# Three late modulation sums moved from VectorE, after the attention, to ScalarE products and adding transfers onto DRAM, during it

## The chip, the cores and the metric

The kernel runs on one core of a Trainium2 chip. The metric is the device time of one launch in microseconds, the median of three runs. The engines are TensorE (PE, with its weight loads as PEld), VectorE (DVE), ScalarE (ACT), GpSimd (POOL) and SyncE (SP), which issues most transfers. Each engine works through its own queue in order.

## The reference

A decoder block on 512 tokens of width 1024, in float32. A conditioning vector gives six modulation rows of 1024 numbers, parts 0 to 5:

```
mod = silu(c) @ w_ada + b_ada
shift1, scale1, gate1, shift2, scale2, gate2 = split(mod, 6)
h = rms_norm(x, g_pre_mix) * (1 + scale1) + shift1
y = token_mixer(h)                      # conv branch, attention branch, gates, w_out
x = x + gate1 * rms_norm(y, g_post_mix)
h = rms_norm(x, g_pre_mlp) * (1 + scale2) + shift2
y = square(relu(h @ w_mlp_in)) @ w_mlp_out
x = x + gate2 * rms_norm(y, g_post_mlp)
```

The token mixer projects h with `w_in`. One branch is a gated unit, a causal depthwise convolution of 31 taps, LayerNorm, swish and `w_conv_out`. The other is attention with eight heads over low-rank queries and keys, then `w_attn_out`. Sigmoid gates merge them and `w_out` follows. Parts 2, 3 and 4 (gate1, shift2, scale2) are what the change is about. They are first used after the output projection.

## The kernel before, in words

Tokens stand in four tiles of 128, the width in eight tiles of 128. Nearly every matrix product is done as three matmuls of high and low halves (`mm3`, line 476), so each weight block that arrives from DRAM is cast on ScalarE and its remainder is formed on VectorE (`W`, line 494). SBUF holds two arenas, `f_arena` (22400 words a partition) and `r_arena` (28000), from which buffers are taken and freed.

The program does not issue instructions as it is written. Helpers record every operation in a planner (line 170; line 410 issues them all, which is why nearly every row of the profile names L410). The planner knows each operation's dependences, a cost, and a due time worked back from TensorE's order (lines 329 to 338). It then plays the engines forward: TensorE keeps the recorded order (moved by `boost`); every other engine takes, whenever it is free, the ready operation with the earliest due time less its `hurry` (lines 345 to 377). An operation may also be tied to an earlier one through `after` (line 318). Transfers are costed at lines 237, 238 and 282 to 286 and 363 to 368; those of GpSimd count double. Buffers are placed by the lives of the plan before it, so a place is used again about 1.5 us after the plan lets it go (`Arena.alloc`, line 90). Up to 14 plans are made and the shortest is issued.

The order of the work: the first modulation and the first gated-unit tiles; the latent projection (`lat_gemm`, line 854); the other gated-unit tiles; the attention (lines 1147 to 1162), where for each head the projection of a later head, the scores of the next and the values of this one alternate; then `w_attn_out`, the second gate, the first gate, the LayerNorm, `w_conv_out`, the output projection, the second modulation and the MLP. The convolution is 248 VectorE steps. `pump` (line 836) records a few at a time among the matrix products: 6 after each piece of the latent projection, 20 after each pair of gated-unit tiles, 7 after each head. GpSimd is used for a few small powers, such as the LayerNorm's (line 1282), and for the adding transfers onto `y_spill` in the MLP (line 1716).

Parts 2, 3 and 4 are summed by `ada_units` (line 1167). A unit is 256 rows of `w_ada` for one part, a load of 1 MB into 2048 words. VectorE multiplies each of its two 128-row halves by a column of `cT` and adds it to an accumulator of 128x1024; a part is four units. What remains, a sum over the 128 partitions, is done in `late_mod` (line 1359): for part 2 by a matmul with ones in `gate_row`, for parts 3 and 4 by transposes and a reduction. The units are drawn by `take` at lines 1239, 1316, 1332 and 1399, in the first gate's product, before the LayerNorm's end and in the merge. Part 5 is summed in the same way in the MLP.

Of the kernel before, what the change touches and what calls it, by code (L numbers as in the profile page):

```python
# [11 lines left out]
F32 = mybir.dt.float32  # L12
# [3 lines left out]
ALU = mybir.AluOpType  # L16

P = 128
T = 512
NT = T // P  # L20
D = 1024
KD = D // P
H = 8
# [17 lines left out]
PUMPS = (6, 10, 7, 6, 5)  # L41
# [8 lines left out]
LEAD = 15000.0  # L50
SLOW = 4000.0
ADAS = (1, 1, 0, 4)
KGRP = ((2,), (3,), (4,), (5,), (6,), (7,))
HX, HA, HG, HC = 1.2e5, 1e5, 3e3, 1.1e5

# [359 lines left out]
def tile_hybrid_block(  # L415
# [12 lines left out]
    out = out[0]  # L428
    w_ada, w_in, conv_w, w_conv_out = w_ada[0], w_in[0], conv_w[0], w_conv_out[0]
# [14 lines left out]
        return tiles[name]  # L444

    hD = [tc.dram_tile([P, KD * T], F32, name=f"h_spill{i}") for i in range(2)]
    yD = [tc.dram_tile([P, D], F32, name=f"y_spill{t}") for t in range(NT)]
    ident = const.tile([P, P], F32, name="ident")
    make_identity(nc, ident)
# [14 lines left out]
    def emit(past, replay):  # L464
        fa = Arena(FT, F_WORDS, past.get("f_arena"), replay.get("f_arena"))
        ra = Arena(RT, R_WORDS, past.get("r_arena"), replay.get("r_arena"))
        pb = Banks(PT, past.get("psum"), replay.get("psum"))
        plan = Planner(nc, dict(f_arena=fa, r_arena=ra, psum=pb))
        pe, act, dve, pool, sp = (plan.engine(e) for e in Planner.NAMES)
# [19 lines left out]
        def load(words, src, pat=None, **kw):  # L489
            b = fa.alloc(words)  # L490
            sp.dma_start(out=fa.v(b, pat, **kw), in_=src)
            return b
# [73 lines left out]
        for t in range(NT):  # L566
            b = fa.alloc(D)
# [268 lines left out]
        def pump(n):  # L836
            for _ in range(n):
                if conv_done[0] >= len(conv_seq):
                    return
                g = next(g for g in CONV_DVE if conv_seq[conv_done[0]] in g)  # L840
                if any(ct not in upad for ct in g):
                    return
                next(conv_it)
                conv_done[0] += 1
# [130 lines left out]
        def rope_half(g):  # L975
            wb = fa.alloc(3 * 4 * DR)
            wv = fa.v(wb, "p (k h c) -> p k h c", k=3, h=4)
            for k in range(3):
                sp.dma_start(out=wv[:, k],
                             in_=w_uq[k * P:(k + 1) * P, :].rearrange("p (h c) -> p h c", c=DN + DR)[:, 4 * g:4 * g + 4, DN:])  # L980
            w = W(fa.v(wb, "p (k n) -> p k n", k=3), 3, 4 * DR)
            fa.free(wb)
            qd = []
            for tp in range(2):
                b = pb.alloc()
                for t in range(2):
                    for k in range(3):
                        mm3(pb.v(b)[:, t * 256:(t + 1) * 256], lat(k, (2 * tp + t) * P, P), w(k, 0, 256), k == 0, k == 2)
                q = fa.alloc(512)
                rope(fa.v(q, "p (m s i) -> p m s i", s=2, i=NR), pb.v(b, 512, "p (t m i) -> p t m i", t=2, i=NR), 2 * tp, 2, 4)  # L990
                pb.free(b)
                qd.append(q)
            w.free()

            for hp in range(2):
                b = pb.alloc()
                for t in range(NT):
                    at = (t % 2) * 256 + hp * P
                    pe.transpose(pb.v(b)[:, t * P:(t + 1) * P], fa.v(qd[t // 2])[:, at:at + P], ident)
                for o in range(2):  # L1000
                    q = ra.alloc(T)
                    me, other = slice(o * DR, (o + 1) * DR), slice((1 - o) * DR, (2 - o) * DR)
                    act.copy(ra.v(q)[me], pb.v(b)[me])
                    dve.tensor_tensor(ra.v(q)[other], pb.v(b)[me], rf(q)[me], ALU.subtract)
                    qst[4 * g + 2 * hp + o] = q
                pb.free(b)
            fa.free(*qd)
# [38 lines left out]
        def proj(h):  # L1046
            pr, o = h // 2, h % 2
            if o == 0:
                weights_pair(pr)
            b = pb.alloc()  # L1050
            for k in range(3):
                mm3(pb.v(b), wq[pr](k, o * DN, DN), lat(k), k == 0, k == 2)
            qh, ql = pair(T)
            split(pb.v(b), qh, ql)
            pb.free(b)
            b = pb.alloc()
            for k in range(2):
                mm3(pb.v(b), wkv[pr](k, o * 256, DN), lat(3 + k), k == 0, k == 1)
            kh, kl = pair(T)
            split(pb.v(b), kh, kl)  # L1060
            pb.free(b)
            qkh[h] = (qh, ql, kh, kl)
            if o == 1:
                wq[pr].free()
            if o == 0:
                v_pair(pr)
            else:
                wkv[pr].free()

        def scores(h):  # L1070
            qh, ql, kh, kl = qkh[h]
            sm = []
            for i in range(NT):
                n = (i + 1) * P
                sl = slice(i * P, n)
                b = pb.alloc()
                o = pb.v(b, n)
                mm3(o, (ra.v(qh)[:, sl], ra.v(ql)[:, sl]), (ra.v(kh)[:, :n], ra.v(kl)[:, :n]), True, False)
                pe.matmul(o, lhsT=ra.v(qst[h])[:, sl], rhs=ra.v(K1)[:, :n], start=False, stop=False)
                pe.matmul(o, lhsT=ra.v(qst[h])[:, sl], rhs=ra.v(K2)[:, :n], start=False, stop=True)  # L1080
                s = fa.alloc(n)
                f = fa.alloc(8)
                fv = fa.v(f)
                dve.tensor_tensor_reduce(fa.v(s), o, mask[:, T - n:], 1.0, 3.0e38, ALU.add, ALU.min, fv[:, 0:1])
                pb.free(b)
                act.activation(fa.v(s), fa.v(s), AF.Exp, scale=-1.0, bias=fv[:, 0:1], accum_out=fv[:, 1:2])
                dve.reciprocal(fv[:, 2:3], fv[:, 1:2])
                act.mul(fa.v(s), fa.v(s), fv[:, 2:3])
                fa.free(f)
                sm.append(s)  # L1090
            ra.free(qst[h])
            ra.free(qh, ql, kh, kl)
            sms[h] = sm
# [50 lines left out]
                else:  # L1144
                    ra.free(vh, vl)

        rope_half(0)
        proj(0)
        proj(1)
        scores(0)  # L1150
        for h in range(H):
            if h + 2 < H:
                proj(h + 2)
            if h == 2:
                rope_half(1)
            if h + 1 < H:
                scores(h + 1)
            pv(h)
            pump(PUMPS[2])
        for q in qkv:  # L1160
            ra.free(*q)
        ra.free(K1, K2)


        ada_acc = {}

        def ada_units(parts):

            for part in parts:
                acc = ada_acc[part] = fa.alloc(D)  # L1170
                for u in range(4):
                    b = fa.alloc(2 * D)
                    v = fa.v(b, "p (j n) -> p j n", j=2)
                    sp.dma_start(out=v, in_=w_ada[u * 256:(u + 1) * 256, part * D:(part + 1) * D].rearrange("(j p) n -> p j n", p=P))
                    for jj in range(2):
                        j = u * 2 + jj
                        if j == 0:
                            dve.tensor_scalar(fa.v(acc), v[:, jj], cT[:, 0:1], None, ALU.mult)
                        else:
                            dve.scalar_tensor_tensor(fa.v(acc), v[:, jj], cT[:, j:j + 1], fa.v(acc), op0=ALU.mult, op1=ALU.add)  # L1180
                    fa.free(b)
                    yield

        def take(it, n=100):
            for _ in range(n):
                if next(it, it) is it:
                    return

        late = ada_units((2, 3, 4))


        def feat_gemm(wsrc, c0, rhs, evac, pumped=0, groups=(2, 2, 2, 2)):
# [41 lines left out]
        def ga_evac(ct, b):  # L1234
            t_ = fa.alloc(T)
            act.activation(fa.v(t_), pb.v(b), AF.Tanh, scale=0.5)
            ta.append(t_)
            if ct % 2:
                take(late, ADAS[2])

        feat_gemm(w_in, C_GB, hs, gb_evac, pumped=PUMPS[4])
        pump(KD * TAPS)
        vT = []
# [69 lines left out]
        plan.boost = 0  # L1313
        feat_gemm(w_in, C_GA, hs, ga_evac)
        free_h()
        take(late, ADAS[3])
        plan.boost = 3000
        layer_norm()
        plan.boost = 0
# [4 lines left out]
        def co_evac(ct, b):  # L1324
            m = fa.alloc(T)
            dve.scalar_tensor_tensor(fa.v(m), fa.v(ta[ct]), 1.0, pb.v(b), op0=ALU.add, op1=ALU.mult)
            dve.tensor_tensor(fa.v(m), fa.v(m), fa.v(yb[ct]), ALU.add)
            hl = pair(T)
            split(fa.v(m), *hl)
            mT.append(hl)  # L1330
            fa.free(m, ta[ct], yb[ct])
            take(late, ADAS[0])

        feat_gemm(w_conv_out, 0, lambda k: (ra.v(vT[k][0]), ra.v(vT[k][1])), co_evac, groups=(4, 2, 2))
        for hl in vT:
# [57 lines left out]
        for k0 in range(0, KD, 2):  # L1393
# [2 lines left out]
                for t in range(NT):  # L1396
                    mm3(pb.v(ys[t, 0]), yl(t, k0 + k), w(k, 0, 512), k0 + k == 0, k0 + k == KD - 1)
            w.free()
        take(late)
        G1 = late_mod()  # L1400
        ys.update({(t, 1): pb.alloc() for t in range(NT)})
        wo = [wunit(w_out, k0, 512, 2, 512) for k0 in range(0, KD, 2)]
# [398 lines left out]
```

## Time and profile before

| | |
|---|---|
| median of 3 runs | 813.99 us (813.33 to 814.12) |
| profiled execution | 812.54 us, of it the span 810.4 us |
| busy PE, DVE | 790.7 us, 738.0 us |
| busy ACT, POOL | 472.0 us, 62.8 us |
| granted TensorE clock | 0.998 |
| moved by DMA | 131.00 MB, mean 162 GB/s |

The profile is one execution. Times inside it count from the span's first instruction. A group row gives engine, operation, what is written and read, shapes and count, then busy time in us and mean ns, then the idle time just before these instructions and what ended most of it. The attention's scores lie at about 166 to 244 us, the LayerNorm's power at 358 us, the loads of `w_ada` for parts 2 to 4 at 346 to 404 us and for part 5 at 633 to 651 us.

### The profile page before, as it was taken

How to read it: one execution, taken by the hardware profiler on the slowest of the kernel's cores; microseconds unless marked ns; L12 is line 12 of the kernel's file. 1: busy time of each engine (PE TensorE's matmuls, PEld its weight loads, DVE VectorE, ACT ScalarE, POOL GpSimd, SP SyncE). 2: the span in 40 equal slices, each digit the busy share in tenths (PEclk: the TensorE clock that was granted, in tenths of full speed). 3: DMA queues.
4: the chain of work that ended last, by engine and by line, in shares of the span. 5: the costliest groups of instructions: out<-in, count | busy, mean ns of one | idle time of the engine just before them, and what ended most of it. 6: DMA issues, size and time to landing. Idle time of an engine off the chain costs nothing. (4 is left out here: it accounts for less than half of the span.)

```text
span 810.4 us, 11974 instructions
## 1 busy us (share of the span) xinstructions
PE 790.7 (98%) x4450; PEld 687.7 (85%) x4450; DVE 738.0 (91%) x1045; ACT 472.0 (58%) x784; POOL 62.8 (8%) x121
## 2 busy tenths in 40 slices
PE   6999999999999999999999999999999999999996
PEld 3778988889897888888888879988998899889985
DVE  3898999999999999999997579899689999996997
ACT  5455463365885247229243378677667756777851
POOL 2001010000000000000000021001002200320023
PEclk9999999999999999999999999999999999999999
DMA  9989433112352160064998044159317991895076
GB/s 295 313 247 341 144 116 110 53 53 66 105 170 78 53 202 5 1 222 162 344 391 281 7 159 148 53 149 266 132 53 157 243 343 37 171 288 178 28 164 134
DMA packets 99981, 131.00 MB, mean 162 GB/s; under 512 B 8433, under 2 KB 67154, under 8 KB 99922
## 3 DMA queue, kind: packets, MB, share of 16 engines
q1 hardware_dynamic: 93586, 118.69, 45.1%
q0 software_dynamic: 6336, 11.54, 8.9%
q8 instruction: 35, 0.57, 0.3%
q14 instruction: 24, 0.20, 0.1%
HBM read 109.23 MB, written 20.97 MB: 161 GB/s over the span
## 5 line engine op out<-in xcount | busy, mean ns | idle before, releaser
L410 PE MATMUL psum<-r_arena 128*128 128x512 f32 (+3 forms) x4108 | 751.1, 344 | 4.0 <-DVE f_arena L410 1.6
L410 PEld LDWEIGHTS psum<-r_arena 128*128 128x128 f32 x4108 | 647.6, 189 | 91.7 <-ACT r_arena L410 2.7
L410 ACT CAST r_arena<-f_arena 128x1024 fp32r<-128x1024 f32 (+5 forms) x249 | 235.2, 966 | 137.3 <-PE psum L410 86.4
L410 DVE TENSOR_TENSOR r_arena<-f_arena,r_arena 128x1024 fp32r<-128x1024 f32 (+5 forms) x259 | 276.1, 1093 | 28.0 <-PE psum L410 15.1
L410 DVE SCALAR_TENSOR_TENSOR f_arena<-f_arena,cw 128x512 f32<-128x512 f32 x240 | 164.2, 737 | 0.0
L410 DVE TENSOR_TENSOR f_arena<-f_arena 128x1024 f32<-128x1024 f32 (+3 forms) x108 | 113.6, 1071 | 4.7 <-ACT f_arena L410 2.4
L410 ACT ACTIVATE f_arena<-f_arena 128x512 f32<-128x512 f32 (+4 forms) x121 | 71.3, 607 | 42.9 <-DVE f_arena L410 42.0
L410 ACT COPY f_arena<-psum 128x512 f32<-128x512 f32 (+4 forms) x103 | 55.3, 547 | 41.5 <-PE psum L410 36.9
L410 DVE SCALAR_TENSOR_TENSOR f_arena<-f_arena,cT 128x256 f32<-128x256 f32 (+1 forms) x70 | 55.9, 800 | 1.2
L410 POOL DMA_DIRECT2D y_spill<-f_arena x40 | 34.8, 879 | 263.6 <-ACT f_arena L410 254.8
L410 ACT ACTIVATE f_arena<-psum 128x512 f32<-128x512 f32 x43 | 25.2, 593 | 45.4 <-PE psum L410 44.3
L410 PE MATMUL psum<-ident,f_arena 128*128 128x128 f32 (+1 forms) x234 | 34.8, 288 | 7.9 <-DVE f_arena L410 7.9
L410 PEld LDWEIGHTS psum<-ident,f_arena 128*128 128x128 f32 (+1 forms) x234 | 28.3, 147 | 14.0 <-DVE f_arena L410 9.3
L410 ACT CAST r_arena<-psum 128x512 fp32r<-128x512 f32 (+2 forms) x57 | 30.0, 562 | 12.7 <-PE psum L410 12.4
L410 DVE TENSOR_TENSOR r_arena<-psum,r_arena 128x512 fp32r<-128x512 f32 (+2 forms) x57 | 35.6, 653 | 0.9 <-ACT r_arena L410 0.6
L410 DVE TENSOR_TENSOR f_arena<-psum,f_arena 128x512 f32<-128x512 f32 (+1 forms) x34 | 22.3, 666 | 7.7 <-PE psum L410 7.6
L410 POOL TENSOR_TENSOR stats<-stats,nhalf 128x1 f32<-128x1 f32 (+1 forms) x17 | 15.5, 915 | 172.3 <-ACT stats L410 156.3
L410 POOL TENSOR_TENSOR lns<-lns,nhalf 128x4 f32<-128x4 f32 x1 | 1.4, 1400 | 249.5 <-DVE lns L410 249.5
L410 ACT ACTIVATE r_arena<-f_arena 128x256 fp32r<-128x256 f32 (+3 forms) x17 | 10.9, 642 | 14.4 <-DVE f_arena L410 11.3
L410 ACT ACTIVATE r_arena<-f_arena,mod 128x512 fp32r<-128x512 f32 x8 | 6.5, 816 | 21.6 <-DVE mod L410 21.6
L410 DVE TENSOR_SCALAR f_arena<-f_arena,stats 128x1024 f32<-128x1024 f32 x8 | 6.0, 753 | 13.6 <-POOL stats L410 13.6
L410 DVE CUSTOM_DVE_ANT_0 f_arena<-psum,mask 128x128 f32<-128x128 f32 (+3 forms) x32 | 14.6, 481 | 0.0
(98 smaller groups left out, 211.1 us busy)
## 6 DMA issues: line engine op xcount, KB each, us to landing
f_arena<-in_w_ada_dram SPq DMA_DIRECT2D x16, 1024.0 KB
f_arena<-in_w_mlp_in_dram SPq DMA_DIRECT2D x32, 512.0 KB
f_arena<-in_w_mlp_out_dram SPq DMA_DIRECT2D x32, 512.0 KB
f_arena<-in_w_in_dram SPq DMA_DIRECT2D x24, 512.0 KB
y_spill<-f_arena POOLq DMA_DIRECT2D x40, 256.0 KB, 6.2
f_arena<-in_w_ada_dram SPq DMA_DIRECT2D x32, 256.0 KB
f_arena<-in_x_dram SPq DMA_DIRECT2D x8, 512.0 KB
h_spill<-r_arena SPq DMA_DIRECT2D x16, 256.0 KB
```

Of the source, the lines that this page charges most:

```text
L410: getattr(self.real[o.eng], o.fn)(*o.a, **o.k)
```

## The change

Parts 2, 3 and 4 are now summed by `ada_sums`, drawn in the attention's loop, one or two units a head (`ADAQ`). A unit is loaded as before. ScalarE multiplies each half in place by its column of `cT`. The first half of a part is stored to a tensor in DRAM (`a_spill`) by SP, and each of the seven others is added onto it there by an adding transfer that GpSimd issues, 512 KB each. The buffer is then freed. A unit's load is tied to the last operation recorded before it, and the unit's operations have 50 us of hurry. Before `late_mod` the three sums are loaded back into SBUF, 512 KB each. The calls of `take` at the four old places are gone; part 5 is left as it was.

```
+ADAQ = (1, 1, 1, 2, 2, 2, 2, 1)
+ADAH = 5e4
...
+    aD = {q: tc.dram_tile([P, D], F32, name=f"a_spill{q}") for q in (2, 3, 4)}
...
+        def ada_sums(parts):
+
+            for part in parts:
+                for u in range(4):
+                    plan.hurry, plan.after = ADAH, len(plan.ops) - 1
+                    b = fa.alloc(2 * D)
+                    v = fa.v(b, "p (j n) -> p j n", j=2)
+                    sp.dma_start(out=v, in_=w_ada[u * 256:(u + 1) * 256, part * D:(part + 1) * D].rearrange("(j p) n -> p j n", p=P))
+                    plan.after = None
+                    for jj in range(2):
+                        j = u * 2 + jj
+                        act.mul(v[:, jj], v[:, jj], cT[:, j:j + 1])
+                        if j == 0:
+                            sp.dma_start(out=aD[part], in_=v[:, jj])
+                        else:
+                            pool.dma_start(out=aD[part], in_=v[:, jj], accum_op=ALU.add)
+                    fa.free(b)
+                    plan.hurry = 0.0
+                    yield
...
-        late = ada_units((2, 3, 4))
+        late = ada_sums((2, 3, 4))
...
             pv(h)
             pump(PUMPS[2])
+            take(late, ADAQ[h])
...
-            if ct % 2:
-                take(late, ADAS[2])
-
...
-        take(late, ADAS[3])
...
-            take(late, ADAS[0])
...
-        take(late)
+        for part in (2, 3, 4):
+            ada_acc[part] = load(D, aD[part])
         G1 = late_mod()
```

More of the change, by code (lines that the diff above doesn't have):

```diff
@@ L1145, in pv @@
                     ra.free(vh, vl)
[L1147 to L1162, printed above, removed]
         ada_acc = {}
@@ L1187, in take @@
                     return
-        late = ada_units((2, 3, 4))
+        late = ada_sums((2, 3, 4))
+        rope_half(0)
+        proj(0)
+        proj(1)
+        scores(0)
+        for h in range(H):
+            if h + 2 < H:
+                proj(h + 2)
+            if h == 2:
+                rope_half(1)
+            if h + 1 < H:
+                scores(h + 1)
+            pv(h)
+            pump(PUMPS[2])
+            take(late, ADAQ[h])
+        for q in qkv:
+            ra.free(*q)
+        ra.free(K1, K2)
         def feat_gemm(wsrc, c0, rhs, evac, pumped=0, groups=(2, 2, 2, 2)):
```

## The prediction

> **What bounds the kernel now.** I read the page first (busy time of each engine), then the busy time by stretches of 25 us from the attention to the second modulation, then who TensorE waited for, and last the groups that the change touches.
>
> ```profile
> PE 790.7 (98%) x4450; PEld 687.7 (85%) x4450; DVE 738.0 (91%) x1045; ACT 472.0 (58%) x784; POOL 62.8 (8%) x121
> ```
>
> TensorE is busy in 98% of the span. A busy PE can still run below its pace, so I look at how many matmuls it gets through. The columns are stretch, length, then busy time and instructions of PE, PEld, DVE, ACT and POOL, the granted clock, the DMA share and GB/s.
>
> ```profile
> 150.00:175.00 25.00, 25.00 (x163) 22.91 (x162) 24.30 (x49) 12.92 (x27) 0.00 (x0) 1.00 0.20 64
> 175.00:200.00 25.00, 24.39 (x158) 21.94 (x157) 25.00 (x60) 17.09 (x40) 0.00 (x0) 1.00 0.14 43
> 200.00:225.00 25.00, 24.79 (x159) 22.09 (x159) 24.77 (x60) 17.40 (x42) 0.00 (x0) 1.00 0.30 95
> 225.00:250.00 25.00, 24.65 (x148) 21.38 (x147) 25.00 (x66) 23.29 (x57) 0.00 (x0) 1.00 0.47 141
> 250.00:275.00 25.00, 25.00 (x111) 20.48 (x110) 24.89 (x36) 7.71 (x10) 0.00 (x0) 1.00 0.29 81
> ...
> 350.00:375.00 25.00, 25.00 (x122) 20.64 (x121) 23.90 (x49) 13.94 (x28) 1.40 (x1) 1.00 0.60 213
> 375.00:400.00 25.00, 25.00 (x112) 20.69 (x111) 24.76 (x30) 14.67 (x22) 0.00 (x0) 1.00 0.78 264
> 400.00:425.00 25.00, 25.00 (x112) 20.72 (x111) 24.82 (x31) 8.86 (x11) 0.00 (x0) 1.00 1.02 383
> 425.00:450.00 25.00, 25.00 (x112) 20.71 (x111) 14.73 (x16) 8.41 (x9) 0.00 (x0) 1.00 0.72 235
> 450.00:475.00 25.00, 24.71 (x125) 20.21 (x125) 16.36 (x22) 10.84 (x30) 3.51 (x5) 1.00 0.11 43
> 475.00:500.00 25.00, 23.34 (x175) 21.93 (x174) 22.58 (x35) 21.66 (x47) 4.30 (x4) 1.00 0.63 212
> ```
>
> ```profile
> L410 PE MATMUL psum<-r_arena 128*128 128x512 f32 x332 | 75.4, 389 | 0.0
> ```
>
> The second fence is PE's only group in 375 to 450: all 512-column matmuls, 332 in 75 us, 226 ns apiece. The stretches show the point on which I build: PE does 112 of them in each of 375-400, 400-425 and 425-450, although VectorE is busy for 24.76 and 24.82 us in the first two and for 14.73 us in the third. There VectorE does not set TensorE's pace. Where PE does stand still is in the attention (0.61 + 0.21 + 0.35 = 1.17 us in 175-250) and after the output projection (0.29 + 1.66 = 1.95 us in 450-500). Whom it waited for there, the attention first:
>
> ```profile
> PE psum L410 <- ACT r_arena L410: 0.8, 2, 0.6
> PE psum L410 <- ACT f_arena L410: 0.3, 1, 0.3
> ```
>
> ```profile
> PE psum L410 <- ACT f_arena L410: 1.1, 1, 1.1
> PE psum L410 <- DVE f_arena L410: 0.5, 2, 0.3
> PE psum L410 <- DVE r_arena L410: 0.3, 1, 0.3
> ```
>
> In the attention it waits for ScalarE, the engine that the change loads.
>
> **What the change removes.** VectorE's products for parts 2, 3 and 4, all between 350 and 430:
>
> ```profile
> L410 DVE SCALAR_TENSOR_TENSOR f_arena<-f_arena,cT 128x1024 f32<-128x1024 f32 x21 | 26.8, 1279 | 0.2
> ...
> L410 DVE TENSOR_SCALAR f_arena<-f_arena,cT 128x1024 f32<-128x1024 f32 x3 | 2.2, 748 | 0.2 <-DMA f_arena<-in_w_ada_dram 0.2
> ```
>
> That is 26.8 + 2.2 = 29.0 us of VectorE. By the three equal stretches it is worth 0 to TensorE; what hides it is PE's own queue of ready matmuls. The twelve 1 MB loads leave this stage too, where the DMA share reaches 1.02, but PE did not stop there either: 0. The waits of 450-500 come from the row norms and the eviction of the transposed h, with VectorE busy only 16.36 and 22.58 of 25 us, and those steps stay. A gain there can only come from the planner's new order; its bound is the 1.95 us, with the attention's 1.17 us 3.1 us in all.
>
> **What it adds to ScalarE.** 24 in-place products of 128x1024 by a column of scalars. The nearest rows are the softmax's scalings and a 1024-wide square:
>
> ```profile
> L410 ACT ACTIVATE f_arena<-f_arena 128x384 f32<-128x384 f32 x16 | 9.8, 612 | 1.1 <-DVE f_arena L410 1.1
> ...
> L410 ACT ACTIVATE f_arena<-f_arena 128x256 f32<-128x256 f32 x16 | 8.0, 501 | 0.9 <-DVE f_arena L410 0.9
> ...
> L410 ACT ACTIVATE f_arena<-f_arena 128x1024 f32<-128x1024 f32 x4 | 4.2, 1061 | 7.4 <-DVE f_arena L410 7.4
> ```
>
> From 501 to 612 ns for 128 more columns is 0.87 ns a column, so 612 + 640 x 0.87 = 1.17 us; the square says 1.06. I take 1.16, near the upper end: 24 x 1.16 = 27.8 us. When they come: a unit's load is tied in the plan to the last operation recorded before it, the convolution step that ends the head's pump. 70 steps are recorded ahead of the attention (5 x 6 in the latent GEMM, 2 x 20 in the GLU loop) and 7 a head, so the heads' ties are steps 77, 84, ... 126. The convolution's VectorE time and steps by stretch (stretch, length, busy and count, clock, DMA, GB/s):
>
> ```profile
> 50.00:75.00 25.00, 1.01 (x3) 1.00 0.85 270
> 75.00:100.00 25.00, 21.04 (x32) 1.00 0.57 200
> 100.00:125.00 25.00, 17.02 (x26) 1.00 0.30 95
> 125.00:150.00 25.00, 15.96 (x24) 1.00 0.39 111
> 150.00:175.00 25.00, 8.95 (x14) 1.00 0.20 64
> 175.00:200.00 25.00, 11.45 (x18) 1.00 0.14 43
> 200.00:225.00 25.00, 7.67 (x11) 1.00 0.30 95
> ```
>
> 85 steps are done by 150, 99 by 175, 117 by 200 and 128 by 225. So heads 0 and 1 release their units before 150, and all twelve are released by about 225. ScalarE's idle time from 150 to 275 is 12.08 + 7.91 + 7.60 + 1.71 + 17.29 = 46.6 us, against 27.8 us to be placed. They fit, but each, once begun, holds back the cast or exponential behind it for up to 1.16 us, and a load that lands late would hold ScalarE's whole queue. The price lies between 0 (all in gaps where ScalarE waits) and 27.8 us (each delays TensorE in full). The planner gives ready attention work its place by due time, PE's own waits there are 1.17 us, and 46.6 is well over 27.8, so I take a value near the low end: 0.5 us, less than half of one product. If that cover goes, see the first rival.
>
> **What it adds to the queues.** SP: the twelve loads move ahead of the reloads of h and the gate weights; three plain stores and, before the second modulation, three 0.5 MB reloads are new. They take SP little, and PE waits for no load in 150-250 above: 0. GpSimd: 21 adding transfers of 512 KB, of which those of one part must wait for each other's landing. Rows: GpSimd's issues now, their landing over the whole run, the queue shares, and the only other thing on GpSimd's queue in this stage, the LayerNorm's power (358.4).
>
> ```profile
> L410 POOL DMA_DIRECT2D y_spill<-f_arena x40: 856/862/1117, 536.2 to 787.0; - x40
> ...
> DMA to landing us min/median/max: 3.6/6.2/9.9
> ```
>
> ```profile
> q1 hardware_dynamic: 93586, 118.69, 45.1%
> q0 software_dynamic: 6336, 11.54, 8.9%
> ```
>
> ```profile
> L410 POOL TENSOR_TENSOR lns<-lns,nhalf x1: 1400/1400/1400, 358.4 to 358.4; 128x4 f32<-128x4 f32 x1
> ```
>
> 256 KB lands in 3.6 to 9.9 us, median 6.2. The adding queue used 8.9% of 810.4 us for 11.54 MB, 6.25 us a MB, so another 256 KB costs 1.6 us: 5.2 us for a piece at the least, 6.2 + 1.6 = 7.8 in the median, 2 x 6.2 = 12.4 if it scales. I take 7.8, since the change itself raises the DMA share: 12.6 MB of loads at 3.08 us a MB (45.1% of 810.4 for 118.69 MB) and 11.0 MB of additions at 6.25 make 108 us over some 165. From about 150 the chain then ends at 150 + 21 x 7.8 = 314, 44 us ahead of the power and over 100 ahead of the reloads. Cost 0, with that margin as its cover.
>
> One rule of the Trainium skill speaks against adding from GpSimd's queue: "SBUF — State Buffer", in its box on the "DVE blocks DMA" trap, says that GpSimd can't write a transfer's descriptors while VectorE runs an instruction in a 2-port mode, and gives about 620 ns alone against about 3100 ns beside a copy. By that page a piece would take 2.5 us more, an estimate of 10.3 us. The trace so far disagrees for this kernel's mix: the 40 issues take 856 to 1117 ns beside a VectorE that is busy for most of that time.
>
> **The sum.** 812.54 us is the profiled execution (span 810.4, 2.1 around it), 1.45 under the median of 813.99. 812.54 - 0 (VectorE) - 0 (DMA) + 0.5 (ScalarE) + 0 (queues) = 813.0, on the median's scale 814.5. A measurement of this kernel can tell about 0.2% from no change, 1.6 us.
>
> **The rivals.** First, slower through ScalarE's order: five of the twelve units (heads 5 to 7) are released in about 198-227, ten products, 11.6 us, where ScalarE has 7.60 + 1.71 = 9.3 us idle from 200 to 250. The overflow of 2.3 us delays the last heads' softmax; if as much is lost in the earlier heads, 4.6 us. 816.3 to 818.6. It decides from two products (2.3 us) that fall straight ahead of what PE waits for. For it: PE's attention waits are all on ScalarE. Against it: 17.29 us of idle time lie just behind, and the planner puts due work first. Chance 0.20.
>
> Second, slower through a buffer: the planner's own rule (lines 282 to 286 and 364 to 366) lets a unit's buffer go 4.9 us after the adding transfer is issued, against my 7.8. Each piece adds 2.9 us of lag, and the next tenant, a load or a softmax tile, waits. One or two such waits on the path: 817 to 820. Chance 0.07.
>
> Third, the chain overruns the LayerNorm. From (358.4 - 150) / 21 = 9.9 us a piece on, the power waits behind additions on GpSimd's queue and all of TensorE with it. At 12.4 us the chain ends at 410, 52 us late, 866; issues that are starved by VectorE lead there as well. By the skill's rule above, 10.3 us a piece would end at 366, 8 us late, about 822. Against it: lone pieces of half the size land in 3.6 us. Chance 0.05.
>
> Fourth, faster: the new order, with more room in the arena and idle VectorE and queues after 350, removes most of the 3.1 us of waits, 810.9 to 812.4. Against it: they hang on ScalarE and the norms, which stay. Chance 0.22. That the planner puts the products behind 250, out of the attention, is possible; there ScalarE is mostly idle, and it gives the forecast.
>
> **How the numbers follow.** No measurable change holds 0.46, its own range 812.4 to 815.6; faster 0.22; slower 0.20 + 0.07 + 0.05 = 0.32. The range 811.0 to 819.0 takes in nearly all of the faster case and the first rival, part of the second, and leaves the third out.
>
> **What would show it.** In the profile after: VectorE about 29 us lighter, all of it in 350-430, while the stretches there still count 112 matmuls; ScalarE about 28 us heavier in 140-275 at 1.1 to 1.2 us a product; PE's idle time in 150-250 near 1.2 to 1.7 us (over 3 says the first rival); additions landing in 5 to 10 us, the last before 330, and the power near 358. I am wrong if VectorE's relief raises PE's count anywhere, if ScalarE waits for a late load in the attention, or if the power is late.

## The result and the profile after

The changed kernel takes 834.85 us (median of 4 runs, 833.90 to 835.78), against 813.97 for the kernel before on the same occasion. The ratio is 1.0258, with a 95% interval from 1.0240 to 1.0276: 2.6% slower, 20.9 us. Its profiled execution took 835.78 us, with a span of 834.0.

The page's first line, busy time of each engine:

```profile
PE 796.3 (95%) x4450; PEld 690.0 (83%) x4450; DVE 713.4 (86%) x1021; ACT 495.6 (59%) x808; POOL 83.5 (10%) x142
```

VectorE is 24.6 us lighter (738.0 before) and ScalarE 23.6 us heavier (472.0), a few us short of the 29 and 28 that were forecast. TensorE's share has fallen from 98 to 95%. The stretches of 25 us show where; the columns are as in the prediction:

```profile
150.00:175.00 25.00, 25.00 (x158) 22.60 (x157) 24.76 (x50) 18.32 (x32) 3.44 (x4) 1.00 0.69 163
175.00:200.00 25.00, 18.36 (x104) 15.98 (x103) 17.30 (x42) 15.40 (x33) 1.72 (x2) 0.86 0.71 164
200.00:225.00 25.00, 25.00 (x169) 22.82 (x168) 24.77 (x57) 19.72 (x42) 2.59 (x3) 1.00 0.74 193
225.00:250.00 25.00, 23.79 (x150) 21.08 (x149) 23.65 (x60) 22.72 (x52) 2.16 (x3) 1.00 0.92 269
250.00:275.00 25.00, 23.74 (x116) 18.21 (x115) 20.92 (x42) 17.36 (x35) 1.30 (x2) 1.00 0.93 278
...
300.00:325.00 25.00, 17.76 (x79) 14.37 (x77) 21.01 (x26) 10.76 (x13) 2.13 (x3) 0.92 0.96 273
...
400.00:425.00 25.00, 25.00 (x112) 20.71 (x111) 8.37 (x9) 10.94 (x15) 0.00 (x0) 1.00 0.52 171
425.00:450.00 25.00, 25.00 (x112) 20.70 (x111) 18.67 (x24) 8.90 (x11) 0.00 (x0) 1.00 0.52 173
450.00:475.00 25.00, 25.00 (x112) 20.68 (x111) 8.41 (x10) 7.30 (x14) 0.00 (x0) 1.00 0.12 39
```

After the LayerNorm TensorE does 112 matmuls a stretch as before, now with a VectorE that is busy for 8.37 us of 25: the relief is there, and TensorE gets no more done for it. The loss is ahead of it. TensorE lacks 6.64 us in 175-200 and 7.24 us in 300-325, and smaller pieces beside them. The two large waits in the list of TensorE's instructions (start, length, then in brackets the idle time and who ended it):

```profile
187.95 8.05 PE L412 MATMUL psum<-r_arena 128*128 128x512 f32 x37 [6.64 <-ACT r_arena L412]
...
325.07 1.11 PE L412 MATMUL psum<-ident,f_arena 128*128 128x128 f32 x4 [7.31 <-ACT f_arena L412]
```

TensorE waits for ScalarE both times. The chain of work through these places (start, length, what) says for what ScalarE waited. The first place:

```profile
173.94 5.06 DMA a_spill<-f_arena
...
179.13 5.43 DMA f_arena<-in_w_ada_dram
...
184.65 2.78 ACT f_arena L412 x4
187.43 0.48 ACT r_arena L412
```

An adding transfer lands at 179.0. Only then is the next unit's load issued, since its place is the buffer that the transfer was reading. ScalarE's next instruction is that unit's product, which stands at the head of its queue until 184.65, with the softmax's exponentials behind it. The adding transfer itself took 5.06 us here, close to the 4.9 us that the planner reckons; by that, what was late is its issue more than its landing, though the planned times are not in the trace to show it. The second place:

```profile
294.18 11.17 DMA f_arena<-in_w_ada_dram
...
305.38 1.16 ACT f_arena L412
...
306.82 8.81 DMA a_spill<-f_arena
...
316.14 8.17 DMA a_spill<-f_arena
...
324.42 0.61 ACT f_arena L412
```

Here ScalarE's eviction of a gate (324.42) writes into a place that an adding transfer still reads, the last but two of the chain. In total for 125 to 345 us (waiter, what ended the wait: us, times, longest), SP's queue first and then ScalarE:

```profile
SPq L412 <- DMA a_spill<-f_arena: 83.2, 12, 16.7
```

```profile
ACT f_arena L412 <- DMA f_arena<-in_w_ada_dram: 23.9, 8, 10.6
...
ACT f_arena L412 <- DMA a_spill<-f_arena: 8.4, 2, 4.6
```

None of the three waits exists in the kernel before. The pieces themselves came out about as sized: the products, the adding transfers with their landing, and the LayerNorm's power.

```profile
L412 ACT ACTIVATE f_arena<-f_arena,cT x24: 1132/1148/1172, 136.2 to 306.4; 128x1024 f32<-128x1024 f32 x24
```

```profile
L412 POOL DMA_DIRECT2D a_spill<-f_arena x21: 856/865/1089, 141.3 to 330.2; - x21
...
DMA to landing us min/median/max: 5.0/7.3/10.6
```

```profile
L412 POOL TENSOR_TENSOR lns<-lns,nhalf x1: 1039/1039/1039, 378.9 to 378.9; 128x4 f32<-128x4 f32 x1
```

The power starts at 378.9 in place of 358.4: 20.5 of the 23.6 us by which the spans differ are lost ahead of it.

### The profile page after: what moved, and what is told of

Same layout as the page of the kernel before. It is cut to its first block, busy times and chain, and to the rows that moved or that the text cites. A ratio compares the mean times of both kernels' runs of the same rounds, so it can differ in the third digit from the quotient of the medians.

```text
span 834.0 us, 12033 instructions
## 1 busy us (share of the span) xinstructions
PE 796.3 (95%) x4450; PEld 690.0 (83%) x4450; DVE 713.4 (86%) x1021; ACT 495.6 (59%) x808; POOL 83.5 (10%) x142
## 4 chain that ended last, share of the span: by engine, by line
PE 64%; DMA 16%; DVE 12%; issue 4%; ACT 3%; POOL 1%; SPq 0%; DVEq 0%; POOLq 0%; ACTq 0%
PE psum L412 64%; DMA f_arena<-in_w_ada_dram 8%; DVE f_arena L412 7%; DVE r_arena L412 5%; DMA a_spill<-f_arena 5%; ACT f_arena L412 2%; DMA f_arena<-in_w_mlp_in_dram 2%; ACT r_arena L412 1%; DMA c<-in_c_dram 1%; POOL stats L412 1%; SPq L412 0%; ACT stats L412 0%; DVE mod L412 0%; DVEq L1817 0%; POOLq L1817 0%
## 5 line engine op out<-in xcount | busy, mean ns | idle before, releaser
L412 PE MATMUL psum<-ident,f_arena 128*128 128x128 f32 x234 | 36.1, 293 | 15.7 <-DVE f_arena L412 7.9
L412 PEld LDWEIGHTS psum<-ident,f_arena 128*128 128x128 f32 x234 | 29.1, 150 | 22.5 <-ACT f_arena L412 10.2
L412 ACT ACTIVATE f_arena<-f_arena,cT 128x1024 f32<-128x1024 f32 x24 | 26.6, 1147 | 23.9 <-DMA f_arena<-in_w_ada_dram 23.9
L412 POOL DMA_DIRECT2D a_spill<-f_arena x21 | 18.3, 874 | 198.7 <-DMA a_spill<-f_arena 70.8
L412 POOL TENSOR_TENSOR stats<-stats,nhalf 128x1 f32<-128x1 f32 (+1 forms) x17 | 19.1, 1128 | 168.1 <-ACT stats L412 158.3
L412 DVE SCALAR_TENSOR_TENSOR f_arena<-f_arena,cT 128x256 f32<-128x256 f32 (+1 forms) x49 | 29.2, 596 | 2.4 <-DMA f_arena<-in_w_ada_dram 1.4
```

The source lines that it names most:

```text
L412: getattr(self.real[o.eng], o.fn)(*o.a, **o.k)
```

## The experiments

Three theories stood at the start. **A**: the planner reckons that an adding transfer lands 4.9 us after its issue and hands its buffer on then; it lands later, and what gets the place waits. **B**: 27 us of products crowd ScalarE. **C**: the added DMA traffic makes the loads late. Each kernel below was timed over several rounds beside the kernel before; its ratio to that kernel is given with its 95% interval.

**No sums at all.** The unit generator is empty.

```
-        late = ada_sums((2, 3, 4))
+        late = iter(())
...
-            ada_acc[part] = load(D, aD[part])
+            ada_acc[part] = load(D, w_ada[0:P, part * D:(part + 1) * D])
```

> Leaves out the sums of parts 2, 3 and 4 altogether: no unit loads, no products, no adding transfers; late_mod gets the first 128 rows of w_ada in their place. It prices VectorE's relief alone, 29 us. All theories: 812 to 816 us, that is no gain, since TensorE did not wait for VectorE there. Under 811 would mean that the relief was worth something after all and was covered by a larger loss.

817.55 us, 1.0054 (1.0035 to 1.0073). With all of the work gone the kernel is 0.5% slower than before, outside what was expected. So VectorE's relief brings no gain, and the new order costs something by itself. Its profile shows the place, behind the output projection. ScalarE's queue there, in this kernel and then in the kernel before:

```profile
474.95 2.94 ACT L412 CAST r_arena<-f_arena 128x1024 fp32r<-128x1024 f32 x3
478.87 0.56 ACT L412 ACTIVATE r_arena<-psum,mod 128x256 fp32r<-128x256 f32 x1 [0.98 <-DVE f_arena L412]
```

```profile
474.02 1.05 ACT L410 CAST r_arena<-f_arena 128x1024 fp32r<-128x1024 f32 x1
474.97 0.56 ACT L410 ACTIVATE r_arena<-psum,mod 128x256 fp32r<-128x256 f32 x1
```

The eviction of the normalized rows starts 3.9 us later. Three weight casts stand ahead of it where it was one, but they are not what it waits for: its row has ScalarE idle for 0.98 us until VectorE is done with a step of the row norm. TensorE's waits just behind it:

```profile
483.25 1.73 PE L412 MATMUL psum<-r_arena 128*128 128x256 f32 x6 [0.92 <-ACT r_arena L412]
487.67 7.91 PE L412 MATMUL psum<-r_arena 128*128 128x256 f32 x48 [0.66 <-ACT f_arena L412]
```

The waits are the smaller part. The stretch 475-500 with all engines, in the prediction's columns, and then TensorE alone in 486-492 (busy time and count, granted clock, DMA share, GB/s):

```profile
475.00:500.00 25.00, 22.47 (x137) 20.07 (x136) 20.06 (x31) 18.13 (x40) 4.18 (x5) 0.86 0.50 169
```

```profile
486.00:492.00 6.00, 5.34 (x25) 0.50 0.55 199
```

TensorE stands still for 2.53 us there against 1.66 before, 0.9 us more; but its granted clock is 0.86 in place of 1.00, which may be worth up to 3.5 us (25 x 0.14, an estimate). So the place is shown. Why the row norm and the clock came out so was not tried. From 350 to 450 TensorE is busy for all 100 us in both kernels, with 453 matmuls in each.

**No adding transfers.** The two lines with `pool.dma_start` and its `else` go.

```
                         if j == 0:
                             sp.dma_start(out=aD[part], in_=v[:, jj])
-                        else:
-                            pool.dma_start(out=aD[part], in_=v[:, jj], accum_op=ALU.add)
```

> Leaves out the 21 adding transfers; the 12 unit loads, the 24 products on ScalarE and the three plain stores stay, so the sums hold one eighth. Theory A (buffers held by adding transfers longer than the planner reckons, the loads and evictions that get their places wait, and ScalarE's queue with them): 812 to 817 us. Theory B (the 27 us of products crowd ScalarE): 830 to 836. Theory C (the added DMA traffic slows the loads): about half of the loss stays, 820 to 826.

817.74 us, 1.0051 (1.0034 to 1.0068): 17 of the 21 us are gone, though all products and all loads are still there. That is 0.7 us above what A gave, under what C gave, and as much as the kernel without any sums. B falls.

**No products.**

```
-                        act.mul(v[:, jj], v[:, jj], cT[:, j:j + 1])
```

> Leaves out the 24 products on ScalarE; the loads, stores and adding transfers stay, so the sums lack the factors. Theory A: ScalarE no longer stands behind late unit loads, but evictions into places that an adding transfer still reads go on waiting: 816 to 828 us, with waits of ScalarE for a_spill transfers and hardly any for w_ada loads. Theory B: 813 to 816. Theory C: 830 to 836.

833.82 us, 1.0251 (1.0233 to 1.0269). The whole loss is there without one product on ScalarE. B falls again, but the number is above what I gave for A and in C's range: I had thought that ScalarE's queue carries most of the loss. The chain of this kernel shows what carries it when ScalarE does not:

```profile
218.08 7.32 DMA a_spill<-f_arena
...
225.68 8.04 DMA a_spill<-f_arena
...
234.01 5.46 DMA a_spill<-f_arena
...
239.48 4.09 DMA f_arena<-in_w_attn_out_dram
...
243.66 1.04 ACT r_arena L412
```

Three adding transfers in series, each behind the other's landing, and then a load of `w_attn_out`, which SP could issue only at 239.48. ScalarE stands 6.62 us idle for that weight; its cast, then a softmax, then the cast for which TensorE waits follow in its queue:

```profile
247.00 7.22 PE L412 MATMUL psum<-r_arena 128*128 128x512 f32 x25 [5.59 <-ACT r_arena L412]
```

So the wait reaches loads that have nothing to do with the sums.

**The right price.** Only the planner's reckoning of an adding transfer onto `a_spill` is raised, by 5 us (`o.late` is 5000 for those and 0 for all else).

```
-                        o.t1 = dma_free + 1100.0
+                        o.t1 = dma_free + 1100.0 + o.late
```

> Same work as the changed kernel; only the planner's reckoning of the landing of an adding transfer onto a_spill is raised by 5 us (from 4.9 to 9.9; measured 5.0 to 10.6, median 7.3). Theory A: buffers are given on later and the next loads are planned later, ScalarE seldom waits for a w_ada load: 813 to 820 us. Theory B and theory C: 830 to 836.

815.12 us, 1.0013 (1.0002 to 1.0025). The work, the traffic and the products are those of the changed kernel, and nearly 20 of the 21 us are gone. C falls, since not a byte was saved. The waits in 125 to 345 us, SP's queue and then ScalarE:

```profile
SPq L413 <- DMA a_spill<-f_arena: 22.4, 4, 15.5
```

```profile
ACT f_arena L413 <- DMA f_arena<-in_w_ada_dram: 10.2, 6, 3.6
```

They were 83.2 and 23.9 us.

**Half the price, and less than the price.** The same edit with 2.5 us, which makes the reckoning 7.4 us, the measured median; and with -1.3 us, which makes it 3.6.

> Same work as the changed kernel; the planner reckons an adding transfer 2.5 us longer, 7.4 us, which is the measured median of 7.3, in place of 4.9. Theory A: most of the loss goes, 814 to 823 us, some stays since half of the transfers land later than that. A theory in which only a margin of several us helps: 826 to 836.

> Same work as the changed kernel; the planner reckons an adding transfer 1.3 us shorter, 3.6 us in place of 4.9. Theory A: the lag of each transfer grows and the loss with it, 836 to 850 us. If the reckoning is not the cause: 830 to 836 or less.

| the planner reckons | time | ratio (95%) |
|---|---|---|
| 3.6 us | 835.72 | 1.0281 (1.0251 to 1.0311) |
| 4.9 us (the change) | 834.85 | 1.0258 (1.0240 to 1.0276) |
| 7.4 us | 821.73 | 1.0111 (1.0078 to 1.0144) |
| 9.9 us | 815.12 | 1.0013 (1.0002 to 1.0025) |

Upwards the loss falls with the reckoning. Downwards it does not grow: 835.72 us lies just under the 836 to 850 that A gave, inside the range for a reckoning that is not the cause, and its interval overlaps that of the change. Where the rest of the loss lies at 7.4 us the profiles show. TensorE from 125 to 350 us at 4.9, 7.4 and 9.9 us (stretch, length, busy time and count, clock, DMA share, GB/s):

```profile
125.00:350.00 225.00, 207.94 (x1111) 0.97 0.74 200
...
125.00:350.00 225.00, 222.93 (x1195) 1.00 0.76 203
...
125.00:350.00 225.00, 223.85 (x1199) 1.00 0.69 186
```

Before the change it was 223.84. At the median of the landings, then, the attention's loss is nearly gone already. The longest wait of that run behind 125 us stands at the LayerNorm:

```profile
364.55 2.03 PE L413 MATMUL psum<-f_arena,ones 128*128 128x128 f32 x16 [2.67 <-issue]
```

What it waits for there the profile does not name. So four values show that the reckoning matters, and not that it must reach the slow end of the landings (10.6).

**Longer lives only.** The planned times stay at 4.9 us; a buffer under an adding transfer counts as held for 15 us more when places are given (`o.late` is 15000 here).

```
-                        end = o.t1 if o.dma else o.t0 + o.cost
+                        end = o.t1 + o.late if o.dma else o.t0 + o.cost
```

> Same work as the changed kernel. Only the lives from which places in the arena are given are made longer: a buffer that an adding transfer onto a_spill reads counts as held for 15 us more; the planned times of the transfers stay at 4.9 us. Theory A1 (places are handed on too early, and the waits for them are the loss): 813 to 820 us, and SP's waits for a_spill fall from 83 us to under 30. Theory A2 (the planned times themselves are the loss, since loads, products and evictions are ordered for adds that land earlier than they do): 826 to 836.

824.26 us, 1.0134 (1.0106 to 1.0161), between the two ranges. SP's wait for the adding transfers is halved, not gone:

```profile
SPq L413 <- DMA a_spill<-f_arena: 41.5, 9, 9.8
```

With places held longer about half of the loss is gone. That the rest comes from an order of the queues made for transfers that land sooner is what A2 says; no run shows it by itself.

**The chain cut.** Units are drawn part by part in turn, so that one unit's adds don't wait for those of the unit before.

```
-            for part in parts:
-                for u in range(4):
+            for u in range(4):
+                for part in parts:
```

> The twelve units are drawn in another order, part by part in turn (2, 3, 4, 2, ...), so that the adds of one unit no longer follow those of the unit before onto the same tensor; only the two of one unit do. The planner reckons as in the changed kernel. Theory A with the serial chain as the source of the lag: 814 to 826 us. Theory A with the length of a single transfer as the source, which the order does not change: 828 to 838.

817.58 us, 1.0054 (1.0032 to 1.0077). The landings are no shorter (5.1 to 10.7 us, median 8.0). What falls is GpSimd's wait for the landing before, here and then in the changed kernel:

```profile
POOL a_spill L412 <- DMA a_spill<-f_arena: 33.2, 7, 9.7
```

```profile
POOL a_spill L412 <- DMA a_spill<-f_arena: 70.8, 11, 8.6
```

So it is not the length of one landing that hurts. SP still waits 58.5 us for adding transfers here, against 83.2, and in the run at 7.4 us it waits only 15.3 us with more of the loss left. The sum of a queue's waits does not size the loss; what counts, by the two chains above, is whether the thing that stands behind a wait is what TensorE needs next.

**Loads on another queue.** The unit loads are issued by GpSimd in place of SP, first without the products, then with them.

```
-                    sp.dma_start(out=v, in_=w_ada[u * 256:(u + 1) * 256, part * D:(part + 1) * D].rearrange("(j p) n -> p j n", p=P))
+                    pool.dma_start(out=v, in_=w_ada[u * 256:(u + 1) * 256, part * D:(part + 1) * D].rearrange("(j p) n -> p j n", p=P))
```

> As the kernel without the products on ScalarE (which took 833.8 us; the sums lack the factors), and the unit loads are issued from GpSimd's queue in place of SP's. If a unit's load that waits at the head of SP's queue for an adding transfer, and holds back the weights behind it, carries that loss: 814 to 824 us. If weight loads and evictions that themselves get places still held by adding transfers carry it: 826 to 836.

> Same work as the changed kernel, products included; only the unit loads are issued from GpSimd's queue in place of SP's, behind the adding transfers there. If SP's queue alone carries the loss: 814 to 820 us. If ScalarE, whose products stand in its queue for loads that come late, carries a part by itself: 822 to 845, with more than 20 us of its waits on w_ada loads, since a load on GpSimd's queue comes later still.

817.38 us, 1.0046 (1.0027 to 1.0065), without the products; 817.28 us, 1.0034 (1.0023 to 1.0044), with them. Either way all but some 3 us of the loss is gone. With the products, the waits of SP's queue and of ScalarE are

```profile
SPq L412 <- DMA a_spill<-f_arena: 26.8, 4, 9.4
```

```profile
ACT f_arena L412 <- DMA f_arena<-in_w_ada_dram: 1.8, 2, 1.4
```

I had expected more waits on ScalarE if it carried a part by itself; there are fewer. Two things changed at once here: SP's queue is free of the units, and the planner counts GpSimd's transfers double, so it also reckons these loads later. How much each brings is not separated.

**No hurry, and both mends.** `ADAH = 0.0` in the changed kernel; and the cut chain together with the right price.

> The changed kernel with the units' 50 us of hurry set to 0, so that other ready work goes first in the plan. Theory A: the reckoning of the adding transfers is as it was, and places are handed on as early, so most of the loss stays: 824 to 836 us. If the hurry is what puts products and loads ahead of the attention's work: 813 to 819.

> Same work as the changed kernel, with both mends: the units drawn part by part in turn, and an adding transfer reckoned 5 us longer. Theory A: 813 to 817 us. It cannot beat the kernel before by more than TensorE's waits there, some 3 us, since VectorE's relief is worth nothing: under 811 would speak against that.

Without hurry 831.27 us, 1.0199 (1.0174 to 1.0224): most of the loss stays, so it is not the units' priority. With both mends 817.60 us, 1.0046 (1.0028 to 1.0064), a little above what I gave and no better than either alone. No version beat the kernel before.

A rival stays beside all of these: each edit makes the planner order and place everything anew, so the change may have met a bad plan by chance. Against it stands that the three versions which keep the adds, their chain, the lives of their buffers and SP's queue as they were, with a reckoning of 4.9 us or below (no products, no hurry, 3.6 us) are all at 831 to 836 us, and the nine others all at 815 to 825.

## Why the prediction was wrong

**VectorE's relief: right.** I gave 0 for 29.0 us less on VectorE. The stretches after the LayerNorm still count 112 matmuls, and the kernel without any sums is not faster.

**ScalarE's products: the price right, the place not.** 1.16 us each was forecast, 1.148 measured. That they crowd the softmax, my first rival, is refuted: with the products and without the adds most of the loss is gone, and without the products it is all there. My own sign for it misled: TensorE's idle time from 150 to 250 is 7.9 us, and "over 3" was to mean the first rival. A sum of idle time does not say what made it.

**GpSimd's pieces: the size right, the end not.** 7.8 us a piece forecast, 7.3 measured; but the chain was to run from 150 to 314 and ran from 141 to 335, 9.2 us a piece. The sum let each piece follow the landing before it, while some also wait for their product, 11.97 us ahead of the one at 306.82. The power did not wait for the chain, so the third rival did not come.

**The step that failed** is "What it adds to the queues", where SP's part was put at 0 ("They take SP little, and PE waits for no load in 150-250 above: 0") and the chain's landing was held only against the LayerNorm and the reloads. I took the count of SP's issues for their price. What counted was what each issue waits for: a buffer that an adding transfer still reads. SP stood for 83.2 us on such landings, ScalarE behind it for 23.9 us on units that came late and for 8.4 us on places directly. The last unit's load was issued at 294.18, where the prediction has all twelve released by about 225. ScalarE's term of 0.5 us leaned on the same 0: it names a late load that would hold ScalarE's whole queue and gives it no price. Two of the three signs that I gave for being wrong came, a late load that ScalarE waits for and a late power.

**The second rival named the mechanism** and had the numbers for it: 4.9 us reckoned against 7.8, a lag of 2.9 a piece, in series. It was given 0.07 and one or two waits, 817 to 820. The count came true: two long waits, 6.64 and 7.31 us, make up 14 of the 16 us that TensorE's idle time gained from 125 to 350 us. The length did not: each is over twice the 2.9 us. All that stands behind the tenant in an in-order queue waits too, from GpSimd to SP to ScalarE to TensorE, and the kernel with the chain cut shows that the serial order of a part's pieces has a share in it. With 3.0 us of lower clock (last section) and 1.3 us more idle time ahead of 125 us the 16 us make some 20 of the 20.5 us by which the power is late.

**A cost that no step held** is that of a new order by itself: 3.9 us in the kernel without sums, most of it at 475-500. The versions without most of the loss end 1 to 4 us above the kernel before, but not through that place: without the adds, at the right price, with the chain cut, with the loads on GpSimd's queue and with both mends the clock in 475-500 is 1.00 and TensorE is busy for 23.3 to 23.7 us, as before. Where they lose it stays open.

## What to carry to other kernels

When an order is planned ahead, a transfer that lands later than planned can cost what stands behind its buffer in every in-order queue, not its own lag alone. Price a new kind of transfer by landings measured in the traffic that it will meet, above all one whose pieces must follow each other (here the median took away 13 of the 21 us, and a value near the slow end nearly all), and ask for each buffer who gets its place next. Before moving work off a busy engine, look at whether the bounding engine's rate differs between a stretch where that engine is full and one where it is not.

## What the runs showed of the hardware

TensorE lost more than its idle time at each of the long waits. TensorE alone, by stretches around the two (stretch, length, busy time and count, granted clock, DMA share, GB/s):

```profile
181.00:188.00 7.00, 0.36 (x3) 0.75 0.81 293
188.00:192.00 4.00, 4.00 (x12) 0.59 0.64 113
192.00:196.00 4.00, 4.00 (x29) 1.00 0.79 123
...
317.00:325.00 8.00, 0.76 (x4) 0.75 1.09 311
325.00:329.00 4.00, 3.93 (x16) 0.65 1.09 264
329.00:335.00 6.00, 6.00 (x34) 1.00 0.56 94
```

In the 4 us after each wait the granted clock is 0.59 and 0.65, and then 1.00 again: 4 x 0.41 + 4 x 0.35 = 3.0 us on top of the waits, an estimate from the clock. The Trainium skill, "TensorE: Matmul & The Clock Gate", Part 1, says that the clock falls to half after an idle window of about 3.4 us and comes back after a busy one of that length; the two waits here, of 6.64 and 7.31 us, agree. The clock was lowered without a long wait as well: in the kernel without sums it was 0.50 from 486 to 492, though no wait of TensorE's near it was over 0.92 us. In the 4 us from 481 to 485 TensorE was busy for 2.41.

On the rule that the prediction weighed, "SBUF — State Buffer" of the Trainium skill on GpSimd's descriptors held back by VectorE: the 21 issues took 856 to 1089 ns, beside a VectorE that was busy for 205 of the 225 us from 125 to 350. Over all runs an issue of an adding transfer took 850 to 1292 ns. No run here shows a hold of the size that the prediction weighed, 2.5 us.
